# A short recurrence moved from beside the prompt's output projection to beside its input projections

## The chip, the cores and the metric

The kernel runs on one core of a Trainium2 chip. The metric is device microseconds of one execution of the whole program. Profiles come from one execution on the chip taken by the hardware profiler; the order of time in them is measured from the first instruction. The engines are TensorE (PE, with its weight loads shown as PEld), VectorE (DVE), ScalarE (ACT), GpSimd (POOL) and SyncE (SP, which here issues most DMAs).

## The reference

A trunk of two layers, applied with the same weights to two groups: a prompt of 1024 rows and a sample of 256 rows, 1024 columns each. In a layer:

```
h = rms_norm(x, norm1_w[l])
proj = h @ w_in[l]                                   # 1024 -> 5 * 640 + 3 * 384 columns
q_h, zf, zb, i_h, g_h, q_a, k_a, v_a = split(proj)
hg_out = hgrn2_mixer(q_h, zf, zb, i_h, g_h, ...)     # 5 heads of 128: S_t = diag(f_t) S_{t-1} + k_t v_t^T,
                                                     # o_t = S_t^T q_t, forward and backward, added,
                                                     # normalised, times silu(g)
at_out = dilated_attention_mixer(q_a, k_a, v_a)      # 3 pairs of heads of 64, windows 128, 512, 2048
x = x + concat([hg_out, at_out]) @ w_out[l]
x = x + expert_choice_moe(rms_norm(x, norm2_w[l]), ...)   # 16 experts, top rows by router affinity
```

and a last norm after both layers. Everything is float32.

## The kernel before

Large products are made of rounded parts: an operand is split into H (rounded on ACT) and L (the rest, a subtraction on DVE), and three products replace one (`mm3`, and as a stream that yields after every second of the eight k chunks, `mm3y`). All matrix instructions go through line 182, all transposes through line 196, all DVE and ACT instructions through line 111, so the profile's groups are told apart by tile names.

A layer has four stages. (1) Projections: the rows are normalised and transposed (`norm_in`; `hTp` for the prompt, `hTs` for the sample), and `project` (L517) walks over seven column blocks of `w_in`, four of 320 columns for values and gates (`value_tile`, L545) and three of 384 for the attention (`qkv_tile`, L558), for both groups; results go to DRAM (`vg`, `qkv`). (2) The prompt's recurrence (`prompt_hgrn`) beside the attention of both groups. (3) The sample's recurrence (`sample_hgrn`, L463) beside the prompt's output projection (`out_proj`, L983), then the prompt's expert choice beside the sample's output projection. (4) The experts.

The recurrence of a head (`hgrn_unit`, L656) projects q and the two gates (24 products each, in units of 512 rows for the prompt, which has ten units, and of 256 for the sample, which has five), then combines chunk sums over seven levels. A level is a group of small products on PE, an update of K, Q and the products of decays (T) on DVE, and a copy (km) on ACT. After the last level (the tile A is filled) the states S are chained, and a tail normalises the head's output and stores it (`mbp` for the prompt, `mbs` for the sample). The weights of a head come in three parts by `load_head` (L593), one part when the part of the head before has been used.

The attention has 30 units, 24 of the prompt and then 6 of the sample; three run at a time, and unit i waits until `int(i * 0.2)` units of the prompt's recurrence have passed their first level (`paced`, L934). `w_out` is split in 16 pieces in the room of `hTp` once the last head is projected (`load_weights`). `out_proj` takes a row tile of 128 rows through loading (`mix`), transposing (`mTh`, `mTl`), 48 products with `oH` and `oL`, the store of x (`xbp`), the norm and the router.

The order of issue is made by streams: Python generators that `lanes` (L134) interleaves. The first stream that is ready in an estimated time goes on; a stream that has work on other engines pending becomes ready when that is estimated to be done. `run_all` runs streams to their ends, `run_until` until some flags are set. From this order, with its own model of the engines, a scheduler fixes the order on each engine and where each tile waits for another. Pools of SBUF lie on a left and a right stack; a tile over another's place waits until that one has been read.

Of the kernel before, what the change touches and what calls it, by code (L numbers as in the profile page):

```python
# [8 lines left out]
F32 = mybir.dt.float32  # L9
# [21 lines left out]
def shape_constants():  # L31
    """Arrays that follow from the shapes alone: rotary tables, masks, slot patterns."""
# [28 lines left out]
def ap_of(a, extra, dims):  # L61
    """The AP of a with its free dims replaced by [stride, count] pairs, extra elements further on."""
    return bass.AP(tensor=a.tensor, offset=a.offset + extra, ap=[list(a.ap[0])] + [list(d) for d in dims])
# [23 lines left out]
class Wait(float):  # L87
    """Yielded by a stream that has nothing to issue for so many ns."""


class Engine:
    """Issues to VectorE or ScalarE and keeps the engine's place in the estimated time."""
# [33 lines left out]
class Body:  # L126
# [6 lines left out]
    # ------------------------------------------------------------------ order of issue  # L133
    def lanes(self, tasks, n=None):  # L134
        """Interleaves streams of instructions, n at a time, first come first.  A stream (made by a task) yields 0
        where it can go on at once, or how long (ns) after the end of what it has issued on the other engines its
        next tensor engine work can start."""
# [23 lines left out]
    def after_all(self):  # L161
        """What follows in this stream depends on all that it has issued since its last yield."""
        self.dep = max(self.dep, self.end)
# [5 lines left out]
    def run_until(self, state, keys, *gens):  # L169
        """Runs the streams until all keys of state are set; those not at their end may go on later."""  # L170
        for d in self.lanes([lambda g=g: g for g in gens]):
            self.clock += d
            if all(state[k] for k in keys):
                break
# [26 lines left out]
    # ------------------------------------------------------------------ helpers  # L201
    def rsqrt(self, ss, n, scale, pool):
        """(ss * scale + eps) ** -0.5 by Newton steps from the exponent's halving."""
# [17 lines left out]
    def rms(self, outs, xs, w_row, pool, junk=None, spare=False):  # L221
        """out = x * rsqrt(mean(x^2) + eps) * w, rows on partitions; the squares go to junk, else to out.  spare: in
        place, with the products on GpSimd and ScalarE."""
# [16 lines left out]
    def transpose_split(self, src, H, L, tp, name="tp"):  # L240
        """Transposes src [128, 1024] into H, L ([128, 8, 128] views, H + L == src^T)."""
        nc = self.nc
        for q in range(2):
            t = tp.tile([P, 4, P], F32, name=name)
            for j in range(4):
                c = (4 * q + j) * P
                self.tr(t[:, j], src[:, c:c + P])
            self.split_from(t, H[:, 4 * q:4 * q + 4], L[:, 4 * q:4 * q + 4])
# [7 lines left out]
    def wblk(self, seg, pools, kc=4, after=None, queues=None):  # L256
        """Loads columns of a [1024, *] matrix, kc k chunks to a tile: (raw, H, L) of [128, kc, N]."""
# [12 lines left out]
    def wparts(self, raws, pools, after=None):  # L270
        """after: instructions that the first parts (H, L) stay behind."""
# [18 lines left out]
    def mm3(self, out, lhs, rhs):  # L290
        """out = sum over 8 k chunks; lhs(k, part), rhs(k, part) give the H (0) or L (1) operand."""
# [6 lines left out]
    def mm3y(self, out, lhs, rhs, order=range(8), stop=True):  # L298
        """mm3 as a stream."""
# [25 lines left out]
    # ------------------------------------------------------------------ program  # L325
    def run(self):
        tc, nc, I, O = self.tc, self.nc, self.I, self.O
        with ExitStack() as ctx:
# [9 lines left out]
            for g, nm in ((gp, "x_prompt"), (gs, "x_sample")):  # L338
# [6 lines left out]
                # the last head's part in halves of its own, ready as soon as each unit is  # L345
# [12 lines left out]
    def next_rows(self):  # L358
        """Room for the sample rows that the next layer begins with."""
# [15 lines left out]
    def constants(self):  # L375
# [5 lines left out]
        # lower bounds: softmax over the two layers, minus its first row after the running sum  # L381
# [18 lines left out]
    # ------------------------------------------------------------------ mixer  # L400
    def mixers(self, l):
        gp, gs = self.groups
        nc, tc = self.nc, self.tc
        pool = self.pool
        with ExitStack() as left, ExitStack() as right:
            hTs = self.new_hT(gs, left.enter_context(pool("hTs")))
            proj = ExitStack()
            hTp = self.new_hT(gp, proj.enter_context(pool("hTp")))
            with pool("rawA", "right") as rw, pool("wA", "right") as wa, \
                    pool("stage", "right") as sp, pool("norm1", "right") as xp:  # L410
                wp = (rw, 3, wa, 4)
# [7 lines left out]
                for i in range(2):  # L419
                    with tc.issue_after(self.scaled.ins if i == 0 else self.lsplit.ins), \  # L420
# [5 lines left out]
                state = dict(normed=0)  # L426
                self.run_all(self.project(l, hTs, hTp, sp, wp, first, state, 2),
                             self.norm_in(l, gp, hTp, xp, w1, junk, state))
# [5 lines left out]
            gp.next, gs.next = gs, None  # L434
            for j in range(3):
                self.load_head(l, gp, 0, j)
# [3 lines left out]
            state = dict(s=0, best=0, started=0, turned=0, multiplied=0, ended=0, projected=0, attended=0, scanned=0, s_scanned=0, loaded=0, p=0, merged=0)  # L440
# [22 lines left out]
            def sample_hgrn():  # L463
                yield from self.until(state, "projected", 1)
                yield from self.until(state, "attended", 1)
                with pool("hgrns") as hg:
                    yield from self.hgrn(l, gs, hTs, hg)
                state["s_scanned"] = 1

            def sample_rest(pools, consts):  # L470
                yield from self.until(state, "s_scanned", 1)
                yield from self.until(state, "p", 8)
                yield from self.out_proj(l, gs, pools, weights[0][1:], consts, state)

            gp.ps, gp.ps_name, gs.ps, gs.ps_name = self.mmp, "mm", self.lvp, "lv"
            hgrns = sample_hgrn()
            with pool("hgrn", "right") as hg:
                loading = load_weights()
                gens = [prompt_hgrn(hg), attention(), hgrns, loading]
                self.run_until(state, ("scanned", "attended"), *[gens[i] for i in (1, 0, 3, 2)])  # L480
            with pool("turned", "right") as tu, pool("normed", "right") as no, pool("mixed", "right") as mi, \
# [3 lines left out]
                gens = [hgrns, self.out_proj(l, gp, pools, weights[0][1:], consts, state),  # L485
                        sample_rest(pools, consts), self.topk_merged(l, gp, no, state), loading]
                self.run_all(*[gens[i] for i in (4, 0, 1, 3, 2)])
# [4 lines left out]
    def norm_in(self, l, g, hT, xp, w1, junk, state):  # L492
        src = g.xin if l == 0 else g.xb
        i0 = 0
        for n in (2, 2, 4):
# [8 lines left out]
            for x in xs:  # L504
# [4 lines left out]
                yield 0.0  # L509

    def blocks(self, l):
        """The column blocks of w_in without the heads' own: (kind, part, columns)."""
# [4 lines left out]
    def project(self, l, hTs, hTp, pool, wp, first, state, ahead):  # L517
        """The column blocks for both groups: the sample runs some blocks ahead, until the prompt is normalised."""
# [11 lines left out]
        for n, (b, g) in enumerate(order):  # L530
            get(b)
            for i in range(g.T):
# [6 lines left out]
                if kind == "v":  # L539
                    self.value_tile(g, hT, parts[b], part, i, pool, nw)  # L540
                else:
                    self.qkv_tile(g, hT, parts[b], part, i, pool)
                yield 0.0

    def value_tile(self, g, hT, blk, b, i, pool, nw):  # L545
        nc = self.nc
        ps = self.mmp.tile([P, 320], F32, name="mm")
        self.mm3(ps, self.top(hT, P * i, P), self.wop(blk, 0, 320))
# [9 lines left out]
    def qkv_tile(self, g, hT, blk, j, i, pool):  # L558
        nc = self.nc
        ps = self.mmp.tile([P, AW], F32, name="mm")  # L560
        self.mm3(ps, self.top(hT, P * i, P), self.wop(blk, 0, AW))
# [16 lines left out]
    def hgrn(self, l, g, hT, pool, after=None, state=None):  # L578
        NU = g.nt // g.unit
        tasks = []  # L580
        state = state or dict(levels=0, first=0, tails=0)
        for h in range(HH):
            hd = dict(h=h, units={}, state=state, after=after if h == HH - 1 else None)
# [9 lines left out]
    def load_head(self, l, g, h, j):  # L593
        """Part j (q, forward z, backward z) of the weights of a head; after a group's last head the next group's."""
# [8 lines left out]
        raw = wp.tile([P, 8, P], F32, name="wr")  # L603
# [5 lines left out]
    def hgrn_task(self, l, g, hd, u, NU, hT, pool):  # L609
# [16 lines left out]
        yield 150.0  # L626
        n = g.unit
# [28 lines left out]
    def hgrn_unit(self, l, g, hd, u, NU, hT, pool):  # L656
# [102 lines left out]
        yield from self.until(state, "tails", (i - 2) // NU + 1)  # L759
        v = pool.tile([P, C, P], F32, name="v", bufs=2)  # L760
# [21 lines left out]
        # chunk sums for the states: S[:, 0, c] before chunk c, S[:, 1, c] after it (backward)  # L782
# [17 lines left out]
    # ------------------------------------------------------------------ attention  # L800
    def attn_units(self, g):
        """(head pair group, query row start and dims, keys, first mask column, window).  Keys: "same" rows as the
        queries, or a list of (name, row start, row stride, count)."""
# [27 lines left out]
    def attention(self, groups, pool, width, scan):  # L831
# [4 lines left out]
        def rows_dma(g, dst, w0, nw, gi, spec):  # L836
            """dst [rows, nw, 128]: qkv parts w0.. of head pair gi at the rows of spec."""
# [96 lines left out]
        def paced(i, u):  # L934
            yield from self.until(scan, "first", int(i * 0.2))
# [5 lines left out]
    # ------------------------------------------------------------------ output projection, norm, router  # L941
    def out_weights(self, l, pool, H, L):
        """w_out as (H, L) of [128, 8, 1024]."""
# [39 lines left out]
    def out_proj(self, l, g, pools, wo, consts, done):  # L983
# [6 lines left out]
        light = g.name == "s"   # VectorE is busy with the prompt's expert choice  # L990

        def row_tile(i):
# [79 lines left out]
            # transposed logits, a part of the k chunks in each quarter of the partitions (in its first 16)  # L1072
            late = light and i == g.T - 1
            if late:    # not in the way of the prompt's expert choice
# [11 lines left out]
            # softmax of the logits r * lg  # L1086
# [23 lines left out]
    # ------------------------------------------------------------------ expert choice  # L1110
    def topk_rounds(self, aff, val, ind):
        """val, ind: the greatest of each row of aff in falling order, first places first; aff is used up."""
# [18 lines left out]
    def topk_merged(self, l, g, pool, done):  # L1131
        """Expert choice over two halves of the tokens: each half's own best, then of A_i and B_(cap-1-i) the greater."""
# [281 lines left out]
```

## Time and profile before

| | |
|---|---|
| median of 3 runs | 3401.52 us (3397.56 to 3407.36) |
| profiled execution | span 3399.2 us, 59013 instructions; mean granted clock 0.978 |
| PE | 3255.7 us (96%) |
| PEld | 2485.4 us (73%) |
| DVE | 2113.0 us (62%) |
| ACT | 1763.4 us (52%) |
| POOL | 270.4 us (8%) |

Layer 0 has its projections from 0 to about 285 us, the prompt's recurrence and the attention until about 690, the sample's recurrence and the output projections between 628 and 905, the experts until 1695; layer 1 repeats this, and the last norm follows from 3356. A product's busy time runs beyond the start of the next one, since products are pipelined; what one costs is read from the distance between starts. Idle time of an engine is what its busy time leaves of a window. The granted clock of PE has two levels, 2.4 GHz (1.00) and 1.2 GHz; a window's figure is a mean.

### The profile page before, as it was taken

To read this page: it belongs to the slowest core of one execution; us is meant where nothing else is said; L and a number is where in the kernel's file an instruction comes from. 1 tells how busy PE (TensorE), PEld (TensorE's weight loads), DVE (VectorE), ACT (ScalarE), POOL (GpSimd) and SP (SyncE) were. 2 spreads that over 40 slices of the span, in tenths; PEclk is the share of its full clock that TensorE was granted. 3 is DMA by queue.
4 is the path that set the end of the run, shared out by engine and by line. 5 is a ranking of instruction groups with operands and counts; after the bars stand their busy time and mean duration, and the time that the engine had idled before them with its cause. 6 is when DMAs were issued, how large, how long until landed. Compare 5 with 4: busy or idle time off the path is not lost.

```text
span 3399.2 us, 59013 instructions
## 1 busy us (share of the span) xinstructions
PE 3255.7 (96%) x23714; PEld 2485.4 (73%) x23714; DVE 2113.0 (62%) x4201; ACT 1763.4 (52%) x2533; POOL 270.4 (8%) x225
## 2 busy tenths in 40 slices
PE   8999999889899999999999999998997999999996
PEld 8998777777666667666699977777775666667664
DVE  5322677885866666666543137788757766666666
ACT  4214774553356666566532156745424665666665
POOL 0000000000111111111100000000001111111102
PEclk9999999899899999999999999998998999999998
DMA  5213222344498889888642132214434988888887
GB/s 180 91 56 89 64 75 60 113 149 127 171 326 281 286 284 323 297 281 284 218 149 89 55 101 67 65 48 134 146 122 170 325 319 287 284 286 312 303 284 251
DMA packets 423969, 641.88 MB, mean 189 GB/s; under 512 B 31376, under 2 KB 191760, under 8 KB 423696
## 3 DMA queue, kind: packets, MB, share of 16 engines
q1 hardware_dynamic: 398544, 557.88, 47.3%
q0 software_dynamic: 24432, 77.61, 8.3%
q8 instruction: 187, 3.06, 0.4%
q10 hardware_dynamic: 720, 2.62, 0.2%
q14 instruction: 86, 0.70, 0.1%
HBM read 551.13 MB, written 86.89 MB: 188 GB/s over the span
## 4 chain that ended last, share of the span: by engine, by line
PE 42%; DVE 3%; DMA 3%; ACT 1%; issue 1%; SPq 0%; POOLq 0%; ACTq 0%; DVEq 0%
PE mm L182 22%; PE lv L182 9%; PE sc L182 6%; PE tp L196 3%; PE tp L182 2%; DMA wr<-in_w_in_dram 1%; DVE wL L111 1%; DMA obr<-obp 0%; ACT wH L111 0%; DVE raw L111 0%; DVE ind L111 0%; DMA xbp<-ye,idxp 0%; DVE val L111 0%; DVE lv L111 0%; DMA xeS<-xns,gidx 0%
## 5 line engine op out<-in xcount | busy, mean ns | idle before, releaser
L111 DVE TENSOR_TENSOR wL<-raw,wH 128x2048 fp32r<-128x2048 f32 (+2 forms) x412 | 917.2, 2244 | 401.6 <-ACT wH L111 401.4
L111 ACT ACTIVATE wH<-raw 128x2048 fp32r<-128x2048 f32 (+2 forms) x412 | 774.4, 1882 | 189.1 <-PE mm L182 92.6
L182 PE MATMUL mm<-wH,hTh 128*128 128x320 f32 (+1 forms) x1120 | 361.1, 323 | 1.4 <-ACT hTh L111 1.3
L182 PE MATMUL mm<-wL,hTh 128*128 128x320 f32 (+1 forms) x1120 | 359.9, 321 | 0.3 <-DVE wL L111 0.3
L182 PE MATMUL mm<-wH,hTl 128*128 128x320 f32 (+1 forms) x1120 | 359.6, 321 | 0.0
L182 PE MATMUL sc<-raw,xs 128*32 128x512 f32 x2048 | 230.9, 597 | 0.0
L182 PEld LDWEIGHTS mm<-wH,hTh 128*128 128x128 f32 x1120 | 210.6, 188 | 2.3 <-ACT hTh L111 2.3
L182 PEld LDWEIGHTS mm<-wL,hTh 128*128 128x128 f32 x1120 | 210.6, 188 | 0.5 <-DVE wL L111 0.5
L182 PEld LDWEIGHTS mm<-wH,hTl 128*128 128x128 f32 x1120 | 210.5, 188 | 0.3 <-DVE hTl L111 0.2
L182 PE MATMUL mm<-wL,xh 128*128 128x512 f32 x512 | 205.3, 401 | 1.6 <-DVE wL L111 1.6
L182 PE MATMUL mm<-wH,xh 128*128 128x512 f32 x512 | 205.4, 401 | 0.0
L182 PE MATMUL mm<-hTh,wH 128*128 128x512 f32 x480 | 203.0, 423 | 0.0
L182 PE MATMUL lv<-wL,xh 128*128 128x512 f32 x512 | 200.1, 391 | 2.1 <-DVE wL L111 2.1
L182 PE MATMUL mm<-wH,xl 128*128 128x512 f32 x512 | 201.1, 393 | 0.0
L182 PE MATMUL lv<-wH,xh 128*128 128x512 f32 x512 | 199.5, 390 | 0.0
L182 PE MATMUL lv<-wH,xl 128*128 128x512 f32 x512 | 199.5, 390 | 0.0
L182 PE MATMUL mm<-hTh,wL 128*128 128x512 f32 x480 | 199.0, 415 | 0.3 <-DVE wL L111 0.3
L182 PE MATMUL mm<-hTl,wH 128*128 128x512 f32 x480 | 196.4, 409 | 0.0
L1264 POOL DMA_INDIRECT xbs<-yS,sidx x64 | 101.8, 1591 | 1120.5 <-ACT yS L111 976.5
L182 PEld LDWEIGHTS sc<-raw,xs 128*32 128x32 f32 x2048 | 64.4, 110 | 147.4 <-issue 144.7
L182 PE MATMUL sc<-raw,hs 128*32 128x512 f32 x1024 | 150.6, 598 | 0.0
L111 DVE TENSOR_TENSOR K<-K,TT 128x256 f32<-128x256 f32 (+1 forms) x360 | 126.1, 376 | 30.1 <-PE lv L182 19.1
(291 smaller groups left out, 6486.0 us busy)
## 6 DMA issues: line engine op xcount, KB each, us to landing
raw<-in_w_up_dram SPq DMA_DIRECT2D x128, 1024.0 KB, 15.6
raw<-in_w_down_dram SPq DMA_DIRECT2D x128, 1024.0 KB, 9.4
raw<-in_w_gate_dram SPq DMA_DIRECT2D x126, 1024.0 KB, 13.8
wr<-in_w_in_dram SPq DMA_DIRECT2D x60, 512.0 KB, 4.0
raw<-in_w_in_dram SPq DMA_DIRECT2D x16, 640.0 KB, 5.7
vgp<-vgo SPq DMA_DIRECT2D x64, 160.0 KB, 1.8
raw<-in_w_in_dram SPq DMA_DIRECT2D x12, 768.0 KB, 5.3
qkvp<-qo SPq DMA_DIRECT2D x48, 192.0 KB, 1.9
```

The source lines that it names most:

```text
L111: return fn(out, *args, **kw)
L182: self.last_mm = self.nc.tensor.matmul(out, lhsT, rhs, start=start, stop=stop)
L196: ins = self.nc.tensor.transpose(out, src, self.ident[:k, :k])
L1264: nc.gpsimd.indirect_dma_start(out=xs2, out_offset=at, in_=yS[64 * h:64 * h + 64], in_offset=None, compute_op=OP.add)
```

## The change

The sample's recurrence leaves stage 3. Once the prompt is normalised (`all_normed`), it runs as a stream of its own beside what is left of `project`, with the first place in the order. Since its values and gates are projected in the same stage, its heads wait for flags: `v` (both value blocks of the sample done) before v is loaded, `g` (both gate blocks) before the tail. `value_tile` and `qkv_tile` become streams (`mm3y` for `mm3`). The sample's heads now come first, and after the last of them `load_head` loads the prompt's first head. The attention's units wait for twice as many units of the prompt's recurrence, ten at most. Pools: `hTp` lies below `hTs`; the raw, weight and staging tiles of the projections go from the right stack to the left, with two raw buffers instead of three; the heads' raw weights use those buffers in stage 1 and a tile of the recurrence's pool in stage 2. Comments and docstrings go, which the diff leaves out.

```diff
     def mixers(self, l):
...
-            hTs = self.new_hT(gs, left.enter_context(pool("hTs")))
-            proj = ExitStack()
+            proj, projs, blk = ExitStack(), ExitStack(), ExitStack()
             hTp = self.new_hT(gp, proj.enter_context(pool("hTp")))
-            with pool("rawA", "right") as rw, pool("wA", "right") as wa, \
-                    pool("stage", "right") as sp, pool("norm1", "right") as xp:
-                wp = (rw, 3, wa, 4)
+            hTs = self.new_hT(gs, projs.enter_context(pool("hTs")))
+            rw, wa, sp = (blk.enter_context(pool(n)) for n in ("rawA", "wA", "stage"))
+            state = dict(normed=0, all_normed=0, v=0, g=0, s=0, best=0, started=0, turned=0, multiplied=0, ended=0,
+                         projected=0, attended=0, scanned=0, loaded=0, p=0, merged=0)
+            wp = (rw, 2, wa, 4)
+            with pool("norm1", "right") as xp:
...
-                state = dict(normed=0)
-                self.run_all(self.project(l, hTs, hTp, sp, wp, first, state, 2),
-                             self.norm_in(l, gp, hTp, xp, w1, junk, state))
+                projecting = self.project(l, hTs, hTp, sp, wp, first, state, 2)
+                self.run_until(state, ("all_normed",), projecting, self.norm_in(l, gp, hTp, xp, w1, junk, state))
...
-            gp.next, gs.next = gs, None
+            self.head_raw = rw, "raw", 2
+            gs.next, gp.next = gp, None
+            gp.ps, gp.ps_name, gs.ps, gs.ps_name = self.mmp, "mm", self.lvp, "lv"
             for j in range(3):
-                self.load_head(l, gp, 0, j)
+                self.load_head(l, gs, 0, j)
+
+            def sample_hgrn():
+                with pool("hgrns", "right") as hg:
+                    yield from self.hgrn(l, gs, hTs, hg, ready=state)
+
+            self.run_all(sample_hgrn(), projecting)
+            blk.close()
+            projs.close()
...
-            def sample_hgrn():
-                yield from self.until(state, "projected", 1)
-                yield from self.until(state, "attended", 1)
-                with pool("hgrns") as hg:
-                    yield from self.hgrn(l, gs, hTs, hg)
-                state["s_scanned"] = 1
-
             def sample_rest(pools, consts):
-                yield from self.until(state, "s_scanned", 1)
                 yield from self.until(state, "p", 8)
...
-            hgrns = sample_hgrn()
             with pool("hgrn", "right") as hg:
+                self.head_raw = hg, "wr", 1
                 loading = load_weights()
-                gens = [prompt_hgrn(hg), attention(), hgrns, loading]
-                self.run_until(state, ("scanned", "attended"), *[gens[i] for i in (1, 0, 3, 2)])
+                gens = [attention(), prompt_hgrn(hg), loading]
+                self.run_until(state, ("scanned", "attended"), *gens)
...
-                gens = [hgrns, self.out_proj(l, gp, pools, weights[0][1:], consts, state),
-                        sample_rest(pools, consts), self.topk_merged(l, gp, no, state), loading]
-                self.run_all(*[gens[i] for i in (4, 0, 1, 3, 2)])
+                self.run_all(loading, self.out_proj(l, gp, pools, weights[0][1:], consts, state),
+                             self.topk_merged(l, gp, no, state), sample_rest(pools, consts))
...
     def norm_in(self, l, g, hT, xp, w1, junk, state):
...
+        state["all_normed"] = 1
...
     def project(self, l, hTs, hTp, pool, wp, first, state, ahead):
...
                 if kind == "v":
-                    self.value_tile(g, hT, parts[b], part, i, pool, nw)
+                    yield from self.value_tile(g, hT, parts[b], part, i, pool, nw)
                 else:
-                    self.qkv_tile(g, hT, parts[b], part, i, pool)
+                    yield from self.qkv_tile(g, hT, parts[b], part, i, pool)
                 yield 0.0
+            if g is gs and b in (1, 3):
+                state["v" if b == 1 else "g"] = 1
...
     def value_tile(self, g, hT, blk, b, i, pool, nw):
...
-        self.mm3(ps, self.top(hT, P * i, P), self.wop(blk, 0, 320))
+        yield from self.mm3y(ps, self.top(hT, P * i, P), self.wop(blk, 0, 320))
...
     def qkv_tile(self, g, hT, blk, j, i, pool):
...
-        self.mm3(ps, self.top(hT, P * i, P), self.wop(blk, 0, AW))
+        yield from self.mm3y(ps, self.top(hT, P * i, P), self.wop(blk, 0, AW))
...
     def load_head(self, l, g, h, j):
...
-        raw = wp.tile([P, 8, P], F32, name="wr")
+        rp, nm, bufs = self.head_raw
+        raw = rp.tile([P, 8, P], F32, name=nm, bufs=bufs)
...
     def hgrn_task(self, l, g, hd, u, NU, hT, pool):
...
         yield 150.0
+        yield from self.until(hd["ready"], "g", 1)
...
     def hgrn_unit(self, l, g, hd, u, NU, hT, pool):
...
         yield from self.until(state, "tails", (i - 2) // NU + 1)
+        yield from self.until(hd["ready"], "v", 1)
         v = pool.tile([P, C, P], F32, name="v", bufs=2)
...
         def paced(i, u):
-            yield from self.until(scan, "first", int(i * 0.2))
+            yield from self.until(scan, "first", min(10, int(i * 0.4)))
             yield from unit(*u)
```

## Rows read from the trace of the kernel before

**Rows 1.** Windows: us; busy and instructions of PE, PEld, DVE, ACT, POOL; clock, DMA, GB/s.

```profile
0.00:285.00 285.00, 273.48 (x1722) 272.47 (x1723) 90.65 (x232) 74.19 (x126) 0.70 (x6) 1.00 0.32 104
285.00:628.00 343.00, 338.73 (x3785) 259.30 (x3784) 232.12 (x728) 209.31 (x464) 6.21 (x8) 0.99 0.26 72
628.00:705.00 77.00, 56.09 (x763) 50.13 (x762) 63.69 (x197) 38.98 (x80) 4.20 (x6) 0.85 0.54 162
705.00:862.00 157.00, 153.07 (x1208) 119.74 (x1207) 100.69 (x417) 63.10 (x154) 10.99 (x19) 0.99 0.40 126
...
1990.00:2313.00 323.00, 320.74 (x3717) 244.16 (x3716) 245.88 (x752) 203.15 (x441) 6.08 (x8) 1.00 0.25 70
2313.00:2388.00 75.00, 54.15 (x732) 47.77 (x731) 65.58 (x201) 38.14 (x77) 3.51 (x5) 0.80 0.49 143
```

**Rows 2.** Groups of PE, 628:862 and 2313:2549: op tiles shapes count | busy, mean | idle.

```profile
L182 PE MATMUL lv<-hTh,wH 128*128 128x256 f32 x120 | 36.6, 305 | 3.1 <-DVE ac L111 2.3 <-ACT K L111 0.8
...
L182 PE MATMUL lv<-hTh,wH 128*128 128x256 f32 x110 | 32.7, 298 | 1.9 <-DVE ac L111 1.3 <-DVE rst L111 0.5
```

**Rows 3.** Order of time on PE, 690:698: start, us, op, tiles, shapes, count.

```profile
690.29 0.28 PE L182 MATMUL lv<-hTh,wH 128*128 128x256 f32 x1
...
690.41 0.28 PE L182 MATMUL lv<-hTl,wH 128*128 128x256 f32 x1
...
696.98 0.33 PE L182 MATMUL lv<-Q,km 128*32 128x32 f32 x16
...
697.25 0.39 PE L182 MATMUL lv<-hTh,wH 128*128 128x256 f32 x1
```

**Rows 4.** Order of time on PE, 523:524, the sample's attention.

```profile
523.50 0.44 PE L182 MATMUL tp<-PT,qkvr 128*64 128x128 f32 x4
523.87 0.33 PE L196 MATMUL tp<-ident,qT 128*128 128x128 f32 x1
```

**Rows 5.** Order of time on POOL: stores of a head's output (mbp) and prompt rows (xbp).

```profile
622.96 0.75 POOL L1108 DMA_DIRECT2D mbp<-hob  x1 [48.26 <-DVE rst L111]
...
687.75 0.75 POOL L1108 DMA_DIRECT2D mbp<-hob  x1 [59.80 <-DVE rst L111]
...
814.93 0.53 POOL L1108 DMA_DIRECT2D xbp<-x  x1 [9.13 <-DVE x L111]
...
861.30 0.53 POOL L1108 DMA_DIRECT2D xbp<-x  x1 [9.21 <-DVE x L111]
...
2376.05 0.78 POOL L1108 DMA_DIRECT2D mbp<-hob  x1 [67.11 <-DMA wr<-in_w_in_dram]
...
2548.47 0.53 POOL L1108 DMA_DIRECT2D xbp<-x  x1 [9.21 <-DVE x L111]
```

**Rows 6.** Order of time on DVE: a prompt unit's Q, and its levels' end (A).

```profile
595.86 1.22 DVE L111 TENSOR_TENSOR Q<-T,qk 128x1024 f32<-128x1024 f32 x1
...
597.74 0.78 DVE L111 COPY_PREDICATED A<-cmask,ac 128x512 f32<-128x512 uint32 x1
...
618.93 0.75 DVE L111 COPY_PREDICATED A<-cmask,ac 128x512 f32<-128x512 uint32 x1
...
628.00 1.23 DVE L111 TENSOR_TENSOR Q<-T,qk 128x1024 f32<-128x1024 f32 x1 [0.30 <-ACT T L111]
...
2313.23 1.22 DVE L111 TENSOR_TENSOR Q<-T,qk 128x1024 f32<-128x1024 f32 x1
```

**Rows 7.** Order of time on PE: the first output products, layers 0 and 1.

```profile
704.32 0.79 PE L182 MATMUL mm<-oH,mTh 128*128 128x512 f32 x1 [0.31 <-ACT mTh L111]
...
704.91 0.63 PE L182 MATMUL mm<-oL,mTh 128*128 128x512 f32 x1
...
2387.77 0.79 PE L182 MATMUL mm<-oH,mTh 128*128 128x512 f32 x1 [0.69 <-ACT mTh L111]
```

**Rows 8.** Chain that ended last, 1670:1730: start, us, what.

```profile
1695.28 9.77 DMA xbp<-ye,idxp
...
1715.03 0.64 PE tp L196 x4
```

More of the change, by code (lines that the diff above doesn't have):

```diff
@@ L87 @@
 class Wait(float):
+    pass
 class Engine:
@@ L433, in mixers @@
             self.wb, self.heads = wb, {}
-            gp.next, gs.next = gs, None
+            self.head_raw = rw, "raw", 2
+            gs.next, gp.next = gp, None
+            gp.ps, gp.ps_name, gs.ps, gs.ps_name = self.mmp, "mm", self.lvp, "lv"
             for j in range(3):
-                self.load_head(l, gp, 0, j)
+                self.load_head(l, gs, 0, j)
[5 more added lines that the diff above has]
+            projs.close()
             weights = []
             scan = dict(levels=0, first=0, tails=0)
-            state = dict(s=0, best=0, started=0, turned=0, multiplied=0, ended=0, projected=0, attended=0, scanned=0, s_scanned=0, loaded=0, p=0, merged=0)
             attn = ExitStack()
@@ L461, in load_weights @@
                 state["loaded"] = 1
-            def sample_hgrn():
-                yield from self.until(state, "projected", 1)
-                yield from self.until(state, "attended", 1)
-                with pool("hgrns") as hg:
-                    yield from self.hgrn(l, gs, hTs, hg)
-                state["s_scanned"] = 1
             def sample_rest(pools, consts):
-                yield from self.until(state, "s_scanned", 1)
                 yield from self.until(state, "p", 8)
                 yield from self.out_proj(l, gs, pools, weights[0][1:], consts, state)
-            gp.ps, gp.ps_name, gs.ps, gs.ps_name = self.mmp, "mm", self.lvp, "lv"
-            hgrns = sample_hgrn()
             with pool("hgrn", "right") as hg:
+                self.head_raw = hg, "wr", 1
                 loading = load_weights()
-                gens = [prompt_hgrn(hg), attention(), hgrns, loading]
-                self.run_until(state, ("scanned", "attended"), *[gens[i] for i in (1, 0, 3, 2)])
+                gens = [attention(), prompt_hgrn(hg), loading]
+                self.run_until(state, ("scanned", "attended"), *gens)
             with pool("turned", "right") as tu, pool("normed", "right") as no, pool("mixed", "right") as mi, \
@@ L576, in qkv_tile, with hgrn @@
                           o.rearrange("p a b -> p (a b)"))
-    def hgrn(self, l, g, hT, pool, after=None, state=None):
+    def hgrn(self, l, g, hT, pool, after=None, state=None, ready=None):
         NU = g.nt // g.unit
@@ L581, in hgrn @@
         state = state or dict(levels=0, first=0, tails=0)
+        ready = ready or dict(v=1, g=1)
         for h in range(HH):
-            hd = dict(h=h, units={}, state=state, after=after if h == HH - 1 else None)
+            hd = dict(h=h, units={}, state=state, ready=ready, after=after if h == HH - 1 else None)
             for u in range(NU):
```

## The prediction

> **What bounds the kernel now.** I read the windows by stage first, then the groups of TensorE instructions in the stretch that the change empties, then the order of time there. TensorE (PE) is the bound nearly everywhere, but not evenly [rows 1]. From 0 to 285 us (projections, layer 0) it is busy 273.5 us, weight loads fill the same time, and VectorE (DVE) is busy 90.7: a stage with room on DVE and none on PE. From 285 to 628 (prompt heads beside attention) PE idles 4.3 of 343 us. From 628, the start of the last prompt unit, to 705, the first product of the output projection, it idles 20.9 of 77 us with DVE at 63.7 and the granted clock at 0.85; the same stretch of layer 1 (2313 to 2388) idles 20.9 of 75 at 0.80. From there to the last prompt row it idles 3.9 of 157. So what rearranging can win is about 25 us of PE idleness per layer and what the half clock costs there; the experts are untouched. The question is whether the stream leaves more PE idleness behind than it removes.
>
> **The change part by part.** All sums are per layer. The base is the profiled execution, span 3399.2 us; the median of the runs is 3401.5, so 2.3 go on top at the end.
>
> *The stream enters the projections.* A sample head has 72 products of 256 columns (360 per layer, a third of them the group of 120 [rows 2]), spaced 0.12 us at full clock [rows 3]: 8.6 us. Its seven groups of small products take 0.27 us each (16 instructions, then the next product) [rows 3], 1.9 us, and 18 instructions of 128 columns about 0.09 each (four small products in 0.37) [rows 4], 1.7 us. That is 12.2 per head, 61 per layer. From above: PE is busy 209 us between 628 and 862 [rows 1], of which eight output tiles at 15.46 [rows 5] are 124, and the last prompt unit's own small products 9 (twice a sample head's 3.6, and the tail of both units); this leaves 76, part of it at half clock. I take **63**, near the full-clock rows, since the projections' granted clock is 1.00. PE is full there, so it comes in whole; the heads' DVE and ScalarE (ACT) work disappears beside it. I add **2.5** for waits of PE inside the stream: the interleaved stage of layer 1 idles 2.3 of 323 us [rows 1]. Bounds 0 and 18; the upper end is the share idle between 628 and 862, a tenth, over half of the longer stage.
>
> *New waits.* `ready` only orders the issue; the planner fills with projection tiles. Two raw buffers instead of three, shared with the heads' 15 parts, delay a load only if ACT or DVE holds one, and both are two thirds idle there. The 15 weight loads and ten loads of v and gates go to SP among the stage's stores, and five stores to POOL, which is empty there; DMA share is 0.32 [rows 1]. The prompt's first tiles lie where the stream and the last blocks lay: ACT waits for their release, and behind it the evacuation of two PSUM tiles, whose 24 products each cover PE. I cost these at nothing; without the cover up to 5 us.
>
> *The attention is paced twice as slowly.* Units 25 to 29, all of the sample, now wait for the last prompt unit's first level, so their PE work leaves the full stretch and falls into the empty one. A unit with one key tile is two transposes, then groups of four, two, four and one at about 0.1 us each [rows 4]: 1.3 us; four of these and one with two key tiles give **-7**. In layer 1, some 30 of the sample's 360 products run before 2313 now (110 of 120 of a third are left after it) [rows 2]: **-3** more.
>
> *What is late next: the last prompt head, alone.* From the last unit's Q (628.00) to the last prompt row's store (861.30) are now 233.3 us, and 235.2 in layer 1 (2313.23 to 2548.47) [rows 5, 6]. Five sample heads run inside. Afterwards that stretch is a chain with little beside it:
> - Q to the finished levels: 23.1 us for the unit before, without sample heads (595.86 to 618.93) [rows 6]. Without its sharers on DVE, 21.
> - Levels to the first store of the head: 25.2 now (597.74 to 622.96) [rows 5, 6], with another unit on DVE in between. I take 20.
> - The clock: granted 0.85 and 0.80 in that window now, and less when it is emptied; 2 more.
> - First store to the first output product: 16.6 in layer 0 (687.75 to 704.32), 11.7 in layer 1 (2376.05 to 2387.77) [rows 5, 7]. The sample's loads no longer share the queue, so 12.
> - Eight rows at 15.46 (three steps from 814.93 to 861.30) [rows 5], 123.7, plus 2 for a start at half clock (the first two products stand 0.59 us apart) [rows 7].
>
> Sum 180.7, so **-52.6** and **-54.5**. Of it 55 lie before the first product, with bounds of 47.7 (19 + 17 + 11.7, all sharers taken out) and 76.4 (59.75 from Q to store as now, plus 16.6). The w_out split, 16 small pieces on ACT and DVE, hides in that window as now; expert choice and the experts follow unchanged.
>
> A rule of the Trainium skill speaks against this part. In the stretch that will be emptied, PE is busy 73% and the grant already falls to 0.85 [rows 1]. TensorE: Matmul & The Clock Gate, Part 1 (The HAM clock gate), says that the throttled clock is the default and that activity releases it; by that rule a window with little PE work would stay throttled throughout and the sum would be 3424 (rival C).
>
> *Start of layer 1.* The weight pool moves to the left, over the last expert's tiles; one lies, by the sizes, over `ye`, which the scatter reads until 1705 (1695.28 + 9.77) [rows 8]. The second half of the first block would wait that long. Cover: prompt rows are not on PE before 1715.03 anyway [rows 8], and the sample's first four tiles need 14 of those 20 us (96 products at 0.15; 1722 instructions in 273.5 us [rows 1]). I take **+2**, between -2 and 8.
>
> **Sum.** Layer 0: 63 + 2.5 - 7 - 52.6 = +5.9. Layer 1: 63 + 2.5 - 7 - 3 - 54.5 = +1.0. With the 2: +8.9, so 3408.1 by the span and **3410** by the median. The gain of a relieved DVE is paid back by the filler that the last head loses.
>
> **The rivals.**
> - *A, the chain alone is quick.* It falls to 47.7 and the rows start warm (-9.3 per layer), the stream costs PE no wait (-2.5), layer 1 starts 2 earlier than summed: 3410 - 25.6 = 3384. For it: DVE was 83% busy in that window [rows 1]. Against it: the 23.1 us already had few sharers.
> - *B, slower: the last head is bound by latency, not by DVE.* It keeps its 59.75 us and the 16.6 to the first product, while nothing fills PE: 202 instead of 180.7 per layer, 3453. It decides from a window of 56 us on, where the sum passes 3412. For it: a chain over three engines. Against it: DVE's queue now carries sample heads in that window.
> - *C, slower: the cold window.* PE is granted half its clock throughout, so the 9 us of its own in the chain take 9 more instead of 2: +7 per layer, 3424. For it: the grant falls where PE idles. Against it: at 73% busy it fell only to 0.85.
> - *D, slower: the projections don't take the stream.* PE waits 18 instead of 2.5 per layer, 3441. Against it: 285 to 628 interleaves the same way with 4.3 idle [rows 1].
>
> **How the numbers follow.** A measurement of this kernel can tell 0.3%, about 10 us, so "same" is 3391 to 3412. Forecast 0.40, own range 3398 to 3424 (0.26 same, 0.14 slower); A 0.30 (0.26 faster, 0.04 same); C 0.10, B 0.12, D 0.08, all slower. That is faster 0.26, same 0.30, slower 0.44. The range 3382 to 3442 leaves out a third of A and most of B.
>
> **What would show it.** The projections grow by 60 to 68 us per layer, with under 5 us of PE idleness inside. From the last unit's Q to the first output product: 50 to 62 us, PE idle over 35 of them, clock under 0.8. Output rows 15.4 us apart with no sample work between. In layer 1's first block PE waits for wL until about 1705. Wrong if that window stays under 45 us or PE finds other work in it (then A), or if PE idles over 10 us per layer in the longer projections (then D).

## The result and the profile after

The changed kernel takes 3483.16 us (median of four runs, 3480.15 to 3485.38) beside 3402.28 of the kernel before: ratio 1.0243, 95% interval 1.0228 to 1.0258. The forecast was 3410, the range 3382 to 3442: wrong, by 73 us.

Windows of the changed kernel, cut where the work changes; columns as in [rows 1]:

```profile
0.00:287.00 287.00, 276.77 (x1760) 275.57 (x1761) 93.50 (x235) 77.32 (x130) 0.70 (x6) 1.00 0.35 112
287.00:418.50 131.50, 111.19 (x1158) 91.85 (x1158) 81.67 (x300) 60.06 (x146) 3.81 (x5) 0.87 0.33 96
418.50:714.00 295.50, 292.33 (x3509) 224.41 (x3507) 218.14 (x670) 173.04 (x376) 6.02 (x8) 1.00 0.22 62
714.00:774.00 60.00, 37.18 (x393) 28.05 (x392) 39.85 (x132) 30.46 (x78) 3.48 (x5) 0.66 0.31 93
774.00:902.00 128.00, 119.92 (x647) 90.25 (x648) 62.61 (x236) 32.02 (x85) 7.62 (x15) 0.96 0.46 142
...
2018.00:2154.00 136.00, 112.35 (x1164) 92.42 (x1163) 88.77 (x323) 60.25 (x146) 3.69 (x5) 0.85 0.32 93
...
2448.00:2506.00 58.00, 37.46 (x392) 28.17 (x392) 39.53 (x131) 29.53 (x75) 3.48 (x5) 0.64 0.31 95
```

The first row should have grown by 60 to 68 us. It holds what [rows 1] have there: 1760 PE instructions in 287 us (1722 in 285), DVE is as idle as before, and the last projection product starts at 286.99 (291.62 in the kernel before, a little behind the cut of [rows 1]). In place of that growth stands a stretch that the kernel before hasn't got (287 to 418.5, and 2018 to 2154), with PE idle for 20 of 131 us and the clock at 0.87. The order of time on PE shows what it is:

```profile
286.81 0.33 PE L182 MATMUL mm<-wL,hTh 128*128 128x384 f32 x1
286.99 0.34 PE L182 MATMUL mm<-wH,hTl 128*128 128x384 f32 x1
287.16 0.28 PE L182 MATMUL lv<-hTh,wH 128*128 128x256 f32 x1
```

The last projection product is followed by the first sample product; all 360 of a layer lie behind it. The stream doesn't run beside the projections: it runs by itself between them and the prompt's recurrence. What PE waits for there (the four largest of its waits from 287 to 371, 13.4 us of 17.0: line, releaser, us in total, times, longest) are the steps of the heads, two of which run at a time, with no other work to go on with:

```profile
PE lv L182 <- ACT km L111: 3.9, 2, 2.8
PE lv L182 <- DVE qk L111: 3.7, 2, 3.3
PE lv L182 <- DVE Q L111: 3.2, 2, 2.4
PE tp L182 <- ACT kt L111: 2.6, 4, 1.5
```

The stretch that the change empties, in the rows that answer to [rows 5 to 7]: the last unit's Q and the end of its levels (DVE), the head's first store (POOL), the first output product (PE), the last prompt row's store (POOL); then the two ends in layer 1.

```profile
714.25 1.22 DVE L111 TENSOR_TENSOR Q<-T,qk 128x1024 f32<-128x1024 f32 x1
...
739.36 0.73 DVE L111 COPY_PREDICATED A<-cmask,ac 128x512 f32<-128x512 uint32 x1
...
766.01 0.75 POOL L1118 DMA_DIRECT2D mbp<-hob  x1 [62.05 <-DVE hob L111]
...
774.11 0.80 PE L182 MATMUL mm<-oH,mTh 128*128 128x512 f32 x1 [0.74 <-ACT mTh L111]
...
901.86 0.53 POOL L1118 DMA_DIRECT2D xbp<-x  x1 [9.21 <-DVE x L111]
...
2447.91 1.22 DVE L111 TENSOR_TENSOR Q<-T,qk 128x1024 f32<-128x1024 f32 x1
...
2634.36 0.53 POOL L1118 DMA_DIRECT2D xbp<-x  x1 [9.21 <-DVE x L111]
```

From Q to the last row it takes 187.6 and 186.5 us, 45.7 and 48.8 less than before. But that Q comes 86.3 us later in layer 0 (628.00 to 714.25) and 96.6 later in layer 1, counted from the last scatter of layer 0 (1695.28 before, 1733.35 after). The loss per layer is the difference, 40.6 and 47.8; what follows the last rows regains 6 us in all (the span grows by 82.3).

**Why the stream stands where it does.** The order of issue says it, and the description of the change ahead of the prediction is wrong there. The first loop runs `project` and `norm_in` until the flag `all_normed` is set. `norm_in` sets it after its last `yield`, so it must be resumed once more, and `lanes` resumes the first ready stream of its list:

```
            ready = [a for a in active if a.ready <= self.clock]
            ...
            lane = ready[0]
```

`project` stands first in that list, and once all rows are normalised it is always ready. `norm_in` gets its last turn when `project` has ended, so "beside what is left of `project`" is beside nothing.

### The profile page after: what moved, and what is told of

It reads as the page before. It is cut to its first block, busy times and chain, and to the rows that moved or that the text cites. A ratio compares the mean times of both kernels' runs of the same rounds, so it can differ in the third digit from the quotient of the medians.

```text
span 3481.5 us, 59076 instructions
## 1 busy us (share of the span) xinstructions
PE 3291.0 (95%) x23714; PEld 2505.4 (72%) x23714; DVE 2128.5 (61%) x4201; ACT 1734.7 (50%) x2511; POOL 270.6 (8%) x225
## 4 chain that ended last, share of the span: by engine, by line
PE 42%; DVE 4%; DMA 2%; ACT 1%; issue 1%; POOLq 0%; ACTq 0%; SPq 0%; DVEq 0%
PE mm L182 22%; PE lv L182 9%; PE sc L182 6%; PE tp L196 3%; PE tp L182 2%; DVE wL L111 1%; DMA obr<-obp 0%; DMA raw<-in_w_in_dram 0%; ACT wH L111 0%; DVE ind L111 0%; DVE Q L111 0%; DVE val L111 0%; DVE raw L111 0%; DVE lv L111 0%; DMA xbp<-ye,idxp 0%
## 5 line engine op out<-in xcount | busy, mean ns | idle before, releaser
L111 DVE TENSOR_TENSOR wL<-raw,wH 128x2048 fp32r<-128x2048 f32 (+3 forms) x448 | 961.0, 2161 | 502.9 <-ACT wH L111 501.7
L111 ACT ACTIVATE wH<-raw 128x2048 fp32r<-128x2048 f32 (+3 forms) x448 | 812.5, 1816 | 249.7 <-PE lv L182 121.4
L111 DVE TENSOR_TENSOR K<-K,TT 128x256 f32<-128x256 f32 (+1 forms) x360 | 124.3, 374 | 38.3 <-PE lv L182 26.7
```

The costliest lines, as they stand in the source:

```text
L111: return fn(out, *args, **kw)
```

## Experiments

**The hand-over** (e1_handover). The flag goes up with the last row. A second edit is then needed: while a head waits in its tail for the gates it holds the one tile of states, S, and by the order of issue the head behind would have reserved that tile ahead of the tail that frees it (no run has the first edit alone).

```
                 i0 += 1
                 state["normed"] = i0
+                state["all_normed"] = i0 == 8
                 yield 0.0
-        state["all_normed"] = 1
...
+        if "S" not in hd and g.name == "s":
+            yield from self.until(state, "tails", h)
         if "S" not in hd:
```

> The changed kernel, but the flag that ends the first loop (all prompt rows normalised) is set with the last row instead of one step later, and a sample head's states wait for the head before. Theory (the loop never handed over, so the stream was issued behind all projections and ran alone): all 120 of a third of the sample products now lie before the last projection product; the last prompt unit's Q comes 28 us earlier in layer 0 and 41 in layer 1 (63 + 2.5 - 7, and 3 less in layer 1, in place of the measured +86.3 and +96.6); 3414 us, 3400 to 3430. Rival 1 (the projections don't take the stream: the two raw buffers are held by the next block nearly all the time): PE idles over 15 us per layer inside the longer projections, 3440 or more. Rival 2 (the loss lies in the pacing of the attention or in the pools): no change from 3483.

Measured: 3416.69 us, ratio to before 1.0031 (1.0017 to 1.0045). Its order of time on PE:

```profile
58.94 0.31 PE L182 MATMUL mm<-wL,hTh 128*128 128x320 f32 x1
59.09 0.31 PE L182 MATMUL mm<-wH,hTl 128*128 128x320 f32 x1
59.32 0.38 PE L182 MATMUL lv<-hTh,wH 128*128 128x256 f32 x1
59.54 0.28 PE L182 MATMUL lv<-hTl,wH 128*128 128x256 f32 x1
59.65 0.31 PE L182 MATMUL mm<-wH,hTh 128*128 128x320 f32 x1
```

Its windows in layer 0:

```profile
0.00:361.00 361.00, 347.93 (x2768) 337.44 (x2769) 172.68 (x515) 121.50 (x240) 4.52 (x11) 1.00 0.36 113
361.00:682.00 321.00, 318.09 (x3657) 243.92 (x3655) 222.39 (x689) 185.21 (x409) 6.04 (x8) 1.00 0.25 69
682.00:740.00 58.00, 33.64 (x395) 24.68 (x392) 39.65 (x132) 30.94 (x78) 3.49 (x5) 0.72 0.32 97
740.00:869.00 129.00, 120.71 (x653) 90.68 (x656) 62.72 (x236) 32.33 (x85) 7.99 (x15) 0.95 0.45 140
```

The sample products, all 360 of layer 0, now stand between the projections'. The first stretch is 74 us longer than in the changed kernel, with PE idle 13.1 us of it (10.2 there, 11.5 in [rows 1]), and the cold stretch behind it is gone. The last Q comes 31.8 and 38.2 us earlier. Two edits of order bring back 66 of the 81 us: the theory held, rival 1 fell (PE has under 3 us more to wait there), and rival 2 too.

**Pacing undone** (e2_pace: `int(i * 0.2)` again).

> The changed kernel with the attention's old pacing (0.2 units of the recurrence per attention unit). Theory (stream alone): the stretch after the projections stays as long; the five late attention units leave the last head's window, where PE idles, so 0 to 14 us slower: 3483 to 3497. Rival 2 (the pacing made the loss): 3410 to 3450.

Measured: 3489.04, ratio 1.0249 (1.0232 to 1.0266), not to be told from the changed kernel's 1.0243: the pacing didn't make the loss. Its windows up to the last Q, and from there to the first output product:

```profile
419.00:724.00 305.00, 299.50 (x3589) 229.63 (x3586) 220.77 (x698) 193.00 (x424) 6.03 (x8) 1.00 0.21 59
724.00:770.00 46.00, 19.60 (x302) 17.20 (x302) 34.39 (x98) 18.97 (x35) 1.73 (x3) 0.60 0.38 116
```

The last head alone needs 45.5 us; with five attention units beside it 59.9. What the full stretch before it saves (10 us in layer 0), it gives back, and PE idles 23 and 26 us there, much the same. About half of that is one wait at the window's end, 12.1 us in the changed kernel and 10.9 in this one: the head's products are done, and PE's next work, the transposing of the first row tile, needs the head normalised, stored and loaded again.

**Without the stream**, in the changed kernel (e3_after_no_stream) and in the kernel before (e4_before_no_stream).

```
-                    yield from self.hgrn(l, gs, hTs, hg, ready=state)
...
+                    nc.vector.memset(zt, 0.0)
+                    for h in range(HH):
...
+                        self.store(mb.rearrange("(c p) e -> p c e", p=P), zt)
```

> The changed kernel without the sample's recurrence (zeros are stored in its place; the prompt's first head is loaded where the sample's was). Theory (stream alone): it takes out the stretch from the last projection product to the first prompt product, 84 and 88 us, so 3305 to 3320. Rival (the stream cost only its PE work): 126 to 131 less, 3352 to 3357. If the rest of the change is neutral, this and the next kernel agree within 15 us.

> The kernel before without the sample's recurrence (zeros are stored in its place). By the prediction's sum the stretch from the last unit's Q to the last prompt row shrinks from 233.3 and 235.2 to 180.7, and in layer 1 three more: 110 less, 3292; with the last head bound by latency (its 59.75 us kept) 3335. Compared with the run before this one it tells what the rest of the change, pacing and pools, is worth without the stream.

Measured: e3_after_no_stream 3268.91, ratio 0.9601 (0.9585 to 0.9617), and e4_before_no_stream 3283.32, ratio 0.9643 (0.9627 to 0.9659). In e3_after_no_stream the first prompt product and the last Q of layer 0:

```profile
287.33 0.39 PE L182 MATMUL mm<-hTh,wH 128*128 128x512 f32 x1
...
608.30 1.22 DVE L111 TENSOR_TENSOR Q<-T,qk 128x1024 f32<-128x1024 f32 x1
```

By the medians the stream costs 3483 - 3269 = 214 us alone behind the projections, 148 beside them (3417 - 3269), and 119 to 122 in the kernel before (110 expected). The expectation for the changed kernel (3305 to 3320) missed: it counted only the stretch up to the prompt's first product, while the prompt's first unit also starts slowly beside the end of the sample's heads: its Q comes 47 us after the first prompt product in the changed kernel (371.4 to 418.5) and 26 without the stream (287.3 to 313.0). The prompt's last Q is at 608.30 without the stream, 106 us earlier. In the kernel before without the stream, Q to the last prompt row is 176.4 us (626.72 to 803.08) where the forecast's sum has 180.7. The other parts of the change are worth 14 us by themselves; which of them was not taken apart. The pacing alone changed no time (e2_pace), and the prompt's first product comes at 287.33 in e3_after_no_stream and at 297.23 in e4_before_no_stream.

**What lies beside the last head.** Three edits of e1_handover: the old pacing; `gens = [prompt_hgrn(hg), attention(), loading]`; no `tensor_tensor(L[at], ...)` in `out_weights`, with `oH` in the place of `oL`.

> The kernel of e1_handover with the attention's old pacing. In the changed kernel the old pacing took the last unit's Q 10 us later and made the stretch from there to the first output product 14 us shorter (59.8 to 45.5), with no change of the time. Theory (work put beside the last head delays that head by about what it saves elsewhere): the same here, 3410 to 3424. Rival (the late attention really fills idle time): 14 us slower, 3431.

> The kernel of e1_handover with the prompt's recurrence ahead of the attention in the list of streams, so that of two ready streams the recurrence is issued first. If the late attention lengthens the last head because it is issued ahead of it, the stretch from the last Q to the first output product falls from 57.6 and 59.3 to 46 to 50 with the last Q where it is: 3390 to 3400. If the order of ready streams doesn't matter there (each step waits for the other engines anyway): 3410 to 3424.

> The kernel of e1_handover without the 16 VectorE instructions that make the low part of w_out (the high part is used twice in the output projection): what the split costs the last head. If VectorE bounds that stretch, it gets shorter by up to the split's 11 us per layer: 3395. The prediction took the split as hidden: no change, 3410 to 3424.

Measured: e5_handover_pace 3412.37, ratio 1.0032 (1.0021 to 1.0044); e6_prompt_first 3411.57, 1.0026 (1.0016 to 1.0035); e7_no_wout_low 3409.28, 1.0024 (1.0014 to 1.0034). None is to be told from e1_handover. The window from the last Q to the first output product, first of e5_handover_pace:

```profile
692.00:737.50 45.50, 18.70 (x302) 16.10 (x302) 34.33 (x98) 18.82 (x35) 1.59 (x3) 0.62 0.37 116
```

The same of e6_prompt_first:

```profile
665.00:745.00 80.00, 57.65 (x503) 38.19 (x504) 48.80 (x186) 44.64 (x137) 3.48 (x5) 0.68 0.38 113
```

The same of e7_no_wout_low:

```profile
683.00:737.50 54.50, 37.40 (x392) 28.11 (x392) 30.47 (x116) 30.43 (x78) 1.92 (x3) 0.66 0.34 104
```

With the prompt first, the attention is pushed to the end: the last Q is 17 us earlier, the window 22 longer, where I had expected it shorter. Without 9 us of DVE work (39.65 to 30.47) the window is 3 us shorter and the rows 2.5 longer, and the last row comes when it did (868.49 and 868.52); in layer 1 the window is 6 us shorter and the last row 3 earlier. The split of w_out on DVE is hidden, as forecast, in layer 0, and in layer 1 but for those 3 us. How much of the window DVE sets stays open: 9 us less of its work make it 3 and 6 us shorter.

**Heads divided** (e8 to e12). The first heads go beside the projections as in e1_handover, the others with the last prompt head and the output rows as before, with the old pacing; hTs stays open below hTp, the heads' raw weights get a pool of their own, and the late stream stands behind `loading` in the lists. e8 has three heads beside, e9 two, e10 four, e12 one; e11 is e8 with a pacing of 0.3.

```
+                    yield from self.hgrn(l, gs, hTs, hg, ready=state, heads=range(3))
...
+            def sample_late():
+                yield from self.until(state, "projected", 1)
+                yield from self.until(state, "attended", 1)
+                ...
+                    yield from self.hgrn(l, gs, hTs, hg, None, dict(levels=3, first=3, tails=3), heads=range(3, HH))
```

> Three sample heads beside the projections (as in e1_handover), the last two issued with the last prompt head and the output rows as in the kernel before, and the attention's old pacing. Theory (work put beside the last head delays it by what it saves): the projections 24 us shorter than in e1_handover, the stretch from the last Q to the last prompt row 20 to 30 longer; 3405 to 3424. Rival (two heads are a filler that PE lacks there): 3380 to 3395, faster than both kernels.

> As e8_three_heads_beside, with two sample heads beside the projections and three late. In that run two late heads took 13 us each out of the projections and made the stretch from the last Q to the first output product 20 longer (45.3 to 65.6) and the rows 5 shorter. If the idle time of TensorE there is used up by two heads, the third costs beside the output rows what it saves before: 3388 to 3400. If there is room for a third: another 6 us per layer less, 3378 to 3385.

> As e8_three_heads_beside, with four sample heads beside the projections and one late. If the gain grows evenly with the late heads: half way between e5_handover_pace and e8_three_heads_beside, 3400 to 3406. If the first late head brings it all (its start keeps TensorE's clock up): 3390 to 3396. If only the second does: 3408 to 3416.

> As e8_three_heads_beside, with the attention paced at 0.3 instead of 0.2. The pacing has moved the time by less than 6 us in the two pairs so far: the same, 3386 to 3400. If attention units near the last heads slow them: slower, over 3400.

> As e8_three_heads_beside, with one sample head beside the projections and four late. From four to two late heads the last prompt head's stretch took up what the projections lost and the time fell (1.0027, 0.9975, 0.9955 of before for one, two and three late heads). If three use up the idle time of TensorE, a fourth only changes places and the time stays, 3385 to 3396; if it delays the last head's chain further, it rises towards the kernel before, where all five are late: 3396 to 3402.

| heads beside the projections | us | ratio to before (95%) |
|---|---|---|
| 5 (e5_handover_pace) | 3412.37 | 1.0032 (1.0021 to 1.0044) |
| 4 | 3414.49 | 1.0027 (1.0018 to 1.0036) |
| 3 | 3392.67 | 0.9975 (0.9965 to 0.9985) |
| 3, pacing 0.3 | 3404.97 | 0.9996 (0.9987 to 1.0006) |
| 2 | 3389.60 | 0.9955 (0.9941 to 0.9968) |
| 1 | 3395.94 | 0.9966 (0.9954 to 0.9978) |

Each ratio is to the kernel before as it was measured along with that run (3400.89, 3405.50 or 3407.27), so the ratios give the order, not the medians. Two heads beside and three late is the fastest measured, 0.45% under the kernel before and so faster than both kernels; its neighbours' intervals overlap with its own, so that one, two and three heads beside can't be told apart. The traces show what each further late head takes off the time of the last Q and what it adds from there to the last row (us, layers 0 and 1; one profile each, against the run with one late head less):

| late head | off the last Q | added behind it |
|---|---|---|
| first (e10) | 11.7, 9.8 | 8.2, 12.7 |
| second (e8) | 15.4, 12.6 | 7.2, 3.5 |
| third (e9) | 16.4, 14.8 | 14.7, 10.1 |
| fourth (e12) | 15.9, 15.9 | 15.0, 12.9 |

Most of the gain came with the second; why with that one isn't shown. Windows of e8, up to the last projection, from the last Q, and from the first output product:

```profile
0.00:335.00 335.00, 320.16 (x2362) 312.50 (x2363) 141.99 (x403) 104.23 (x196) 3.07 (x9) 1.00 0.35 112
...
665.00:731.00 66.00, 46.37 (x696) 40.08 (x695) 57.70 (x195) 33.21 (x73) 4.21 (x6) 0.83 0.46 143
731.00:856.00 125.00, 121.25 (x661) 90.79 (x662) 63.76 (x250) 34.62 (x90) 8.38 (x16) 0.98 0.43 135
```

The same of e9:

```profile
0.00:319.00 319.00, 306.28 (x2163) 300.91 (x2164) 126.15 (x347) 94.85 (x174) 2.33 (x8) 1.00 0.35 111
...
649.00:724.00 75.00, 57.04 (x779) 51.54 (x778) 61.76 (x197) 36.92 (x80) 4.20 (x6) 0.84 0.46 139
724.00:854.00 130.00, 123.93 (x789) 92.85 (x784) 72.89 (x305) 38.63 (x104) 9.00 (x16) 1.00 0.45 137
```

In layer 0, two late heads take 25 us from the projections (their last product starts at 335.56, 360.82 in e5), add 20 to the window (45.2 to 65.6) and shorten the rows by 5 (130.0 to 125.1): of the 25 us, 15 are paid again. My theory that such work gives back what it saves held for the attention and for the first late head, nearly for the third and fourth, and fell for the second. The pacing of 0.3 made e11 slower than e8 by 0.2%, where I had expected no change: its last Q is 5.7 us later in layer 0; in layer 1 it is 4.8 earlier, but the stretch behind it is 6 longer.

## Why the prediction was wrong, by its own steps

- **"The stream enters the projections", 63 + 2.5 per layer: this step failed.** I costed the stage as the text of the change describes it and never walked the order of issue through the hand-over, though all its lines were in the diff and in the kernel. "`ready` only orders the issue; the planner fills with projection tiles" was assumed. Alone, the stream costs 106 us in layer 0 (last Q at 608.30 without it, 714.25 with it). An estimate from the window of 287 to 418.5 gives most of that: some 65 us of PE work, 20 of idle PE, and 17 for the clock (13% of 131.5). Of the excess 13 came back because the other edits bring that Q 19.7 us forward (628.00 to 608.30), where I had counted 7: some 9 by the pacing, and 10 because the prompt's first product comes sooner, which the sum had at nothing. Where it does enter, 65.5 was near: in e1_handover the sample's products and small groups take 64.9 us of PE (sum of the distances between starts, layer 0), PE waits 2.7 more, and the projections' own products take 6.4 longer (267.3 to 273.8), which I hadn't counted: 74 in all.
- **Rival D had the place but not the price.** "The projections don't take the stream" was given 18 us of PE waits per layer, from an interleaved stage. The stream isn't interleaved at all, and the price is that of two heads at a time by themselves, 106 us where D had 81. Its sign, longer projections with idle PE in them, didn't show.
- **The last head, 180.7 us: right within 7** (187.6 and 186.5). Q to levels 25.1 (21 forecast), levels to store 26.7 (20), store to product 8.1 (12), rows 127.8 (125.7). The excess is the attention's: without it Q to product takes 45.5 and Q to the last row 176.3 (e2_pace), against 55 forecast and 59.9 measured for the former. The sum moved the late units there and put what they cost the chain at nothing; they cost it 14 us.
- **Attention, -7: a wash.** The units leave the full stretch (last Q 9.8 us earlier in e1_handover than in e5_handover_pace) and lengthen the window by 12; the sum had the first half alone.
- **Rival A's 47.7 us for a quick chain** was right for a head without neighbours (45.5 and 44.2 in e2_pace), rival B's threshold of 56 us was passed (59.9 and 58.3) but not its 202 us to the last row reached, and neither made the loss: beyond the forecast's sum the stretch from the last Q to the last row adds 7 and 6 us, what lies before that Q 28 and 39.
- **Rival C.** The clock in the emptied window fell to 0.66 and 0.64, from 0.85 and 0.80 [rows 1], and to 0.60 with less beside the head (e2_pace), as the Trainium skill has it ("TensorE: Matmul & The Clock Gate", Part 1 (The HAM clock gate)): activity releases the clock. It wasn't throttled throughout, which would be 0.50.
- **Start of layer 1, +2:** its first projection product comes 2.9 us after the last scatter is issued (1733.35 to 1736.22), 0.5 before (1695.28 to 1695.77). The size is right and the reason isn't: that product waits for wH (2.1 us) and the next for wL (1.0, to 1737.75), neither until the scatter's end at 1739.66.
- **The whole sum.** With the hand-over mended the kernel takes 3416.69 where the sum gave 3410: 1.0031 of before, forecast 1.0025. That is near in part by luck: in layer 0 the stream takes 74 us instead of 65.5 and the last stretch 186.0 instead of 180.7, while the other edits bring 19.7 instead of 7. The working was near for another order of issue than the one that the kernel has.

## What to carry to other kernels

Where streams set the order, follow the hand-over step by step: a flag set behind a stream's last yield waits for one more turn of that stream, and a scheduler that takes the first ready one may not give it until the other has ended. After such a move look first at the first start of what was moved: one row (287.16, behind the last projection) tells it. In this kernel work moved into the full projections cost its whole length and somewhat more (65.5 us counted, 74 taken); beside the last head, whose steps leave PE idle, it cost anything from a quarter of that to somewhat more than all. How much goes to each is worth measuring head by head.

## What the hardware showed beyond expectation

With the hand-over mended, eight sample products of layer 0 follow a projection product: three of them held PE for 0.22 us (one from 59.32 to 59.54), the others for 0.12 to 0.14, where 0.12 lie between its like [rows 3]. Interleaving made the projections' own products 2.4% longer than in the changed kernel. The kernel after also loses by the clock: over the whole run the mean granted clock is 0.964, 0.978 before and 0.975 with the hand-over mended.
